# Moving the start of the output weights, the convolution's closing norm and two attention steps in a hybrid decoder trunk

## The chip, the cores and the metric

The kernel runs on one core of one Trainium2 chip. The metric is the device time of one execution in microseconds (us). Of several runs the median is taken.

## What is computed

The reference is a trunk of two layers over x of 512 positions by 1024 features. Each layer adds half a SwiGLU feed-forward part, then a mixer, then half a second feed-forward part:

```python
for l in range(DEPTH):                                   # DEPTH = 2
    x = x + 0.5 * swiglu(rms_norm(x, ffn1_norm[l]), ...)  # 1024 -> 2816 -> 1024
    h = rms_norm(x, mix_norm[l])
    a, g, q, k, v = jnp.split(h @ w_in[l], splits, axis=-1)       # 512 columns each
    conv_out = conv_module(a, g, conv_w[l], conv_b[l], conv_norm[l])
    ...
    diff_out = diff_attention(q, k, v, rel_bias, lam, lam_init, subln_norm[l])
    x = x + jnp.concatenate([conv_out, diff_out], axis=-1) @ w_out[l]
    x = x + 0.5 * swiglu(rms_norm(x, ffn2_norm[l]), ...)

def conv_module(a, g, conv_w, conv_b, conv_norm):
    u = a * jax.nn.sigmoid(g)
    y = <causal depthwise convolution of u, width 31> + conv_b
    return jax.nn.silu(rms_norm(y, conv_norm))            # norm over the 512 channels

def diff_attention(q, k, v, ...):     # 4 heads, two maps of width 64 each, values of width 128
    # per block of 128 queries: s = q k / sqrt(d) + bias, causal; p = softmax(s)
    a = p[:, :, 0] - lam * p[:, :, 1]
    o = a @ v;  o = rms_norm(o, subln_g) * (1.0 - lam_init)
```

## The kernel before

All matrix products are made in three passes of a shorter float format. A number is split into a high part (a copy in that format) and a low part (the number less its high part), and a product is high by high, low by high and high by low, added in one bank of PSUM. The helper `mm3` issues the three (L172, L175, L176). For the weights, `chunk` loads 512 KB with a DMA of SyncE's queue into a slot of the ring `wraw` (five slots), and `parts_of` has ScalarE make the high part (`whi`, L100) and VectorE, or GpSimd where the call names it, the low part (`wlo`, L101); each of these rings has four slots. x lies feature by feature in eight tiles of 128 features by 512 positions.

The eight banks of PSUM are shared out by tag: two for `mm`, two for `sc`, two for `po`, one for `tp`, one for `y`. A scheduler orders the instructions of each engine after the program is written; only instructions handed to `tc.keep_in_program_order` keep their places among each other. So the order of the calls below is a wish, and the built order can differ.

The mixer of a layer goes so:

- `conv_in` makes the four channel tiles `us[c]` of the convolution (a tile is 128 channels by 512 positions), and `project` and `to_features` make keys `kt` and queries `qz`.
- `project_values(j)` makes the values of 128 positions with 24 matmuls (L630 to L632), four such blocks; ScalarE scales them into `vv` (L633).
- `conv_taps(c, n)` does the 31 taps of channel tile c. Of these, n are made by ScalarE (products, L671) and GpSimd (sums, L672), the rest by VectorE (L686), by `POOL_TAPS = (31, 0, 0, 10)`. VectorE joins both parts (L689), and `conv_square` adds the squares into `csum` (ScalarE L658, GpSimd L659).
- `attend(n)` is a pipeline over 16 steps, four blocks of 128 queries from the last to the first, with four heads each. At call n, step n makes two score matmuls (L717, in banks `sc` and `po`; 512, 384, 256 or 128 columns wide), VectorE adds the bias and takes the minimum (L721), ScalarE the exponentials (L725), and VectorE joins both maps (L728, L730, L731). Step n - 2 is transposed (TensorE L738, ScalarE L740), step n - 3 multiplied with the values (L747). With the last head of a block come its norm (`se` L754, ScalarE L756, VectorE `so` L758, GpSimd L759 and the root L223, VectorE `ov` L762), and with step n - 5 its way out (`block_out`: transposes L774, high part L776, low part L777).
- `conv_finish` closes the convolution branch: `rows_rstd` turns the channel sums into rows (TensorE L230, VectorE L234, L235, GpSimd's root L223), `spread` copies them to all partitions (TensorE L243, ScalarE `rb` L247); then for each channel tile GpSimd multiplies (L697), ScalarE takes tanh (L699), VectorE forms the swish (L700), ScalarE the high part `acth` (L701) and VectorE the low part `actl` (L702).
- The output projection multiplies half 0 (the conv channels) for all eight output tiles of 512 columns, then half 1 (attention) in two parts of 256 columns. The results take the banks `sc` and `po` in turn, after the scores, and VectorE adds them to x (L828). The weights come by `chunk(wout[l, half, m // 2], G)`: their low parts are GpSimd's.

What decides the order around the change is written in the mixer's last part:

```python
for n in range(2):
    attend(n)
    project_values(NT - 1 - 2 * n)
    project_values(NT - 2 - 2 * n)
for c in range(CT):
    conv_taps(c, POOL_TAPS[c])
for n in range(2, len(steps) + 5):
    attend(n)
conv_finish()
```

## Time and profile before

| what | value |
|---|---|
| median of 3 runs | 1792.57 us (1792.52 to 1795.35) |
| the profiled execution's own time | 1792.75 us |
| its span | 1791.0 us |
| granted TensorE clock | 1.00 |
| TensorE busy | 1783.5 us |
| VectorE busy | 1203.1 us |
| ScalarE busy | 895.0 us |
| GpSimd busy | 643.1 us |

The span is the stretch of the profiled execution from its first to its last instruction; the time beside it also has what lies around it. A row of a timeline gives the start in us from the start of the span, the duration in us, the engine, the line and operation, the tile written and those read, the shape and the count of instructions taken together; in brackets stand the idle time before it and what ended it. PE is TensorE, DVE is VectorE, ACT is ScalarE, POOL is GpSimd. Matmuls overlap in the pipeline, so their pace is read from start to start. Instructions of the other engines overlap by some hundredths of a us too. Line numbers in the rows are those of the kernel before.

### The profile page before, as it was taken

Reading aid. Unit: us, or ns where it says so; the run is one execution under the profiler, and the core shown is the slowest. Engines: PE = TensorE matmul, PEld = TensorE weight load, DVE = VectorE, ACT = ScalarE, POOL = GpSimd, SP = SyncE. Lnnn points to the kernel's source line nnn. Section 1 sums busy time; section 2 is a strip of 40 time slices with the busy share of each in tenths; the row PEclk is TensorE's granted clock in tenths of the full one; section 3 lists DMA queues with packets and bytes.
Section 4 is the critical chain, followed back from the end, with each engine's and each line's share of the span. In section 5 each row is a group of like instructions: output and inputs, shape, how many; then the busy total and the mean of one; then the engine's idle time right before and its main releaser. Section 6 shows DMA issues by size and latency. Waiting matters only on the chain.

```text
span 1791.0 us, 28372 instructions
## 1 busy us (share of the span) xinstructions
PE 1783.5 (100%) x10861; PEld 1591.8 (89%) x10861; DVE 1203.1 (67%) x1849; ACT 895.0 (50%) x1479; POOL 643.1 (36%) x453
## 2 busy tenths in 40 slices
PE   9999999999999999999999999999999999999999
PEld 7899899888788899899888998998887888998997
DVE  7877476568867767477566665765788587674762
ACT  6455265445845455265433643654558354552651
POOL 2242232269843133133102412312798331322420
PEclk9999999999999999999999999999999999999999
DMA  7366466322212367367333654663231133664651
GB/s 247 107 174 185 112 179 175 119 93 94 71 48 84 94 165 191 104 171 193 102 95 99 169 168 121 174 182 118 71 116 50 48 107 96 169 172 112 182 150 59
DMA packets 111721, 231.24 MB, mean 129 GB/s; under 512 B 12151, under 2 KB 33414, under 8 KB 111584
## 3 DMA queue, kind: packets, MB, share of 16 engines
q1 hardware_dynamic: 91488, 191.93, 33.5%
q0 software_dynamic: 19808, 37.33, 12.5%
q8 instruction: 85, 1.39, 0.3%
q14 instruction: 52, 0.43, 0.1%
q10 hardware_dynamic: 288, 0.16, 0.0%
HBM read 227.26 MB, written 3.42 MB: 129 GB/s over the span
## 4 chain that ended last, share of the span: by engine, by line
PE 95%; DVE 4%; DMA 0%; issue 0%; ACT 0%; SPq 0%; DVEq 0%; ACTq 0%
PE ps_pair L384 38%; PE ps_d L172 9%; PE ps_d L176 9%; PE ps_d L175 9%; PE ps_pair L176 5%; PE ps_pair L175 5%; PE ps_pair L172 5%; PE ps_pair L601 2%; PE ps_pair L600 2%; PE ps_pair L602 2%; PE ps_out L175 1%; PE ps_out L176 1%; PE ps_out L172 1%; PE ps_sc L717 1%; DVE actl L261 1%; PE ps_v L632 1%
## 5 line engine op out<-in xcount | busy, mean ns | idle before, releaser
L100 ACT ACTIVATE whi<-wraw 128x512 fp32r<-128x512 f32 (+2 forms) x600 | 466.0, 801 | 611.3 <-PE ps_pair L384 226.4
L101 DVE TENSOR_TENSOR wlo<-wraw,whi 128x512 fp32r<-128x512 f32 (+2 forms) x557 | 521.6, 959 | 219.6 <-ACT whi L100 214.6
L384 PE MATMUL ps_pair<-acth,wlo 128*128 128x256 f32 x1088 | 308.3, 283 | 0.0
L384 PE MATMUL ps_pair<-actl,whi 128*128 128x256 f32 x1088 | 308.3, 283 | 0.0
L384 PE MATMUL ps_pair<-acth,whi 128*128 128x256 f32 x1088 | 308.3, 283 | 0.0
L175 PE MATMUL ps_d<-hl,whi 128*128 128x512 f32 x704 | 274.3, 390 | 0.0
L176 PE MATMUL ps_d<-hh,wlo 128*128 128x512 f32 x704 | 273.1, 389 | 0.0
L172 PE MATMUL ps_d<-hh,whi 128*128 128x512 f32 x704 | 269.3, 390 | 0.0
L384 PE MATMUL ps_pair<-th,wlo 128*128 128x256 f32 x816 | 231.2, 283 | 0.0
L384 PE MATMUL ps_pair<-tl,whi 128*128 128x256 f32 x816 | 231.1, 283 | 0.0
L384 PE MATMUL ps_pair<-th,whi 128*128 128x256 f32 x816 | 231.1, 283 | 0.0
L150 POOL DMA_DIRECT2D wraw<-in_gu x68 | 81.9, 1204 | 412.9 <-DMA wraw<-in_gu 143.2
L155 POOL TENSOR_TENSOR wraw<-wraw 128x512 f32<-128x512 f32 x68 | 104.9, 1543 | 331.0 <-DMA wraw<-in_gu 239.8
L384 PEld LDWEIGHTS ps_pair<-acth,whi 128*128 128x128 f32 x1088 | 209.1, 192 | 0.3
L384 PEld LDWEIGHTS ps_pair<-actl,whi 128*128 128x128 f32 x1088 | 209.1, 192 | 0.3
L384 PEld LDWEIGHTS ps_pair<-acth,wlo 128*128 128x128 f32 x1088 | 209.1, 192 | 0.0
L484 DVE SCALAR_TENSOR_TENSOR x<-ps_d,x 128x512 f32<-128x512 f32 x96 | 64.8, 689 | 179.0 <-PE ps_d L176 178.7
L175 PE MATMUL ps_pair<-actl,whi 128*128 128x512 f32 x448 | 175.0, 391 | 0.3 <-DVE actl L261 0.2
L176 PE MATMUL ps_pair<-acth,wlo 128*128 128x512 f32 x448 | 174.6, 391 | 0.0
L172 PE MATMUL ps_pair<-acth,whi 128*128 128x512 f32 x448 | 174.0, 393 | 0.2 <-ACT whi L100 0.2
L384 PEld LDWEIGHTS ps_pair<-th,whi 128*128 128x128 f32 x816 | 156.7, 192 | 0.6
L384 PEld LDWEIGHTS ps_pair<-tl,whi 128*128 128x128 f32 x816 | 156.7, 192 | 0.7
(169 smaller groups left out, 3247.1 us busy)
## 6 DMA issues: line engine op xcount, KB each, us to landing
wraw<-in_gu SPq DMA_DIRECT2D x208, 256.0 KB, 4.0
wraw<-in_gu SPq DMA_DIRECT2D x104, 512.0 KB, 3.7
wraw<-in_gu POOLq DMA_DIRECT2D x68, 512.0 KB, 5.7
wraw<-in_wqkv SPq DMA_DIRECT2D x24, 512.0 KB, 3.6
wraw<-in_dn SPq DMA_DIRECT2D x84, 128.0 KB, 3.0
wraw<-in_dn SPq DMA_DIRECT2D x32, 256.0 KB, 3.2
wraw<-in_wag SPq DMA_DIRECT2D x16, 512.0 KB, 3.6
wraw<-in_wout SPq DMA_DIRECT2D x16, 512.0 KB, 3.6
```

What stands on the lines that cost most here:

```text
L100: S.activation(hi, raw, AF.Copy)
L101: (eng or V).tensor_tensor(out=lo, in0=raw, in1=f32(hi), op=ALU.subtract)
L150: nc.gpsimd.dma_start(two.rearrange("p (b c) -> p b c", b=2), u[:, h[0]].unsqueeze(1).broadcast_to([P, 2, 512]), accum_op=ALU.add)
L155: G.tensor_tensor(more[:, h[0]], two[:, h[1]], whole[:, h[0]], op=ALU.add)
L172: first = T.matmul(ps, wh, xh, start=start, stop=False)
L175: T.matmul(ps, wh, xl, start=False, stop=False)
L176: T.matmul(ps, wl, xh, start=False, stop=stop)
L384: mm = T.matmul(ps, l, r, start=first and i == j == 0, stop=False, skip_group_check=True)
L484: V.scalar_tensor_tensor(x[:, m, :], ps, 0.5, x[:, m, :], op0=ALU.mult, op1=ALU.add)
L600: T.matmul(ps[n], xh[:, t], wh, start=k == 0, stop=False)
L601: T.matmul(ps[n], xh[:, t], wl, start=False, stop=False)
L602: T.matmul(ps[n], xl[:, t], wh, start=False, stop=k == KT - 1)
```

## The change

In the changed kernel:

- The calls of `attend` and `project_values` alternate otherwise: the third step (`attend(2)`) comes ahead of the last value block, the fourth (`attend(3)`) behind it and ahead of the conv taps.
- The first four chunks of the output weights (half 0) are asked for by `next_wo`, with low parts on GpSimd that are kept in program order: the first inside `conv_taps` of the last channel tile (behind its taps), the second behind `rows_rstd`, the third and fourth behind `conv_finish`.
- `rows_rstd` for the conv norm is called ahead of `attend(4)`, and `conv_finish` behind `attend(8)`, instead of both at the end.
- The tanh result goes into the PSUM bank `y` instead of an SBUF tile.
- `se` is made by ScalarE (a square with a scale) instead of VectorE.

With the added lines, the lines of the mixer move down by 2 to 19: L697 becomes L701, L699 L703, L700 L704, L702 L706, L717 L721, L828 L847.

```diff
@@ -93,17 +93,19 @@
         dt = F32 if "raw" in tag else F32R
         return wp.tile([P, n], dt, tag=tag, name=tag, bufs=RING[tag])
 
-    def parts_of(raw, hi, lo, eng=None, first=False):
+    def parts_of(raw, hi, lo, eng=None, first=False, pin=False):
         if first:
             V.tensor_scalar(hi, raw, 1.0, None, op0=ALU.mult)
         else:
             S.activation(hi, raw, AF.Copy)
-        (eng or V).tensor_tensor(out=lo, in0=raw, in1=f32(hi), op=ALU.subtract)
-
-    def chunk(src, eng=None):
+        low = (eng or V).tensor_tensor(out=lo, in0=raw, in1=f32(hi), op=ALU.subtract)
+        if pin:
+            tc.keep_in_program_order(low)
+
+    def chunk(src, eng=None, pin=False):
         raw, hi, lo = ring("wraw"), ring("whi"), ring("wlo")
         nc.sync.dma_start(raw, src)
-        parts_of(raw, hi, lo, eng)
+        parts_of(raw, hi, lo, eng, pin=pin)
         return hi, lo
 
     def by_halves(src):
@@ -658,7 +660,7 @@
                     S.activation(sq, y, AF.Square)
                     G.tensor_tensor(csum, csum, sq, op=ALU.add)
 
-            def conv_taps(c, n):
+            def conv_taps(c, n, then=None):
 
                 wc = _AT["conv_w"] + c * TAPS
                 yp = None
@@ -685,17 +687,19 @@
                 for t in range(n + 1 if n else 1, TAPS):
                     V.scalar_tensor_tensor(ys[c] if t == PAD and not n else y, us[c][:, t : t + SEQ],
                                            pars[l][:, wc + t : wc + t + 1], y, op0=ALU.mult, op1=ALU.add)
+                if then is not None:
+                    then()
                 if n:
                     V.tensor_tensor(ys[c], y, yp, op=ALU.add)
                 conv_square(c, ys[c])
 
-            def conv_finish():
-                rcv = spread(rows_rstd(csum, CC, "c")[0], "rb")
+            def conv_finish(rcv):
+                rcv = spread(rcv, "rb")
                 for c in range(CT):
                     z = ys[c]
                     hg = ghalf[l][:, c : c + 1]
                     G.tensor_tensor(z, z, rcv, op=ALU.mult)
-                    th = mt.tile([P, SEQ], F32, tag="gl", name="th", bufs=1)
+                    th = bank("y", "ps_th")
                     S.activation(th, z, AF.Tanh, scale=hg)
                     V.scalar_tensor_tensor(z, th, 1.0, z, op0=ALU.add, op1=ALU.mult)
                     S.activation(ch[:, c, :], z, AF.Copy, scale=hg)
@@ -751,7 +755,7 @@
                 po = pos[i]
 
                 se = small.tile([P, HEADS], F32, tag="se", name="se")
-                V.scalar_tensor_tensor(se, sums[i][:, 0, :], VD * EPS, sums[i][:, 0, :], op0=ALU.mult, op1=ALU.mult)
+                S.activation(se, sums[i][:, 0, :], AF.Square, scale=math.sqrt(VD * EPS))
                 sq = tmp.tile([P, SEQ], F32, tag="sq", name="sq")
                 S.activation(sq, po, AF.Square)
                 so = small.tile([P, HEADS], F32, tag="so", name="so")
@@ -803,21 +807,36 @@
             nc.sync.dma_start(bias, skew[0])
             row["bias"] = bias
 
-            for n in range(2):
+            attend(0)
+            project_values(3)
+            project_values(2)
+            attend(1)
+            project_values(1)
+            attend(2)
+            project_values(0)
+            attend(3)
+
+            wo = []
+
+            def next_wo():
+                wo.append(chunk(wout[l, 0, len(wo)], G, pin=True))
+
+            for c in range(CT):
+                conv_taps(c, POOL_TAPS[c], next_wo if c == CT - 1 else None)
+            rcv = rows_rstd(csum, CC, "c")[0]
+            next_wo()
+            for n in range(4, len(steps) + 5):
                 attend(n)
-                project_values(NT - 1 - 2 * n)
-                project_values(NT - 2 - 2 * n)
-            for c in range(CT):
-                conv_taps(c, POOL_TAPS[c])
-            for n in range(2, len(steps) + 5):
-                attend(n)
-            conv_finish()
+                if n == 8:
+                    conv_finish(rcv)
+                    next_wo()
+                    next_wo()
 
 
 
             for half, t in ((0, slice(0, SEQ)), (1, slice(SEQ // 2, SEQ)), (1, slice(0, SEQ // 2))):
                 if t.stop == SEQ:
-                    w = [None] * 4
+                    w = [None] * 4 if half else wo
                 for m in range(KT):
                     if w[m // 2] is None:
                         w[m // 2] = chunk(wout[l, half, m // 2], G)
```

## The prediction

> **What bounds the kernel now.** I read the page first, then busy time by windows, then the timelines of the engines around the one place where TensorE waits.

> ```profile
> span 1791.0 us, 28372 instructions
> PE 1783.5 (100%) x10861; PEld 1591.8 (89%) x10861; DVE 1203.1 (67%) x1849; ACT 895.0 (50%) x1479; POOL 643.1 (36%) x453
> PE 95%; DVE 4%; DMA 0%; issue 0%; ACT 0%; SPq 0%; DVEq 0%; ACTq 0%
> ```

> TensorE is busy all along and carries 95% of the chain that ended last; VectorE carries 4%. The change takes no matmul away, so it can gain only where TensorE runs below its rate. The windows show where (columns: window, us, then PE, PEld, DVE, ACT, POOL busy, clock, DMA share, GB/s):

> ```profile
> 470.00:484.00 14.00, 14.00 (x72) 9.85 (x71) 9.34 (x30) 12.72 (x29) 13.59 (x9) 1.00 0.52 150
> 484.00:511.00 27.00, 25.89 (x157) 20.55 (x156) 26.33 (x93) 22.45 (x67) 12.40 (x13) 1.00 0.01 2
> 1373.00:1400.00 27.00, 25.88 (x157) 20.51 (x156) 25.98 (x94) 22.71 (x68) 12.55 (x14) 1.00 0.02 7
> ```

> From 484 to 511 of layer 0, and at the same place of layer 1, VectorE is full (26.33 of 27.00): attention's masks and differences share it with the end of the convolution branch. Just before, it is a third idle while GpSimd is full (13.59 of 14.00). How far TensorE falls back is read from its steps, start to start:

> ```profile
> 471.45 1.88 PE L717 MATMUL ps_sc<-kt,qz 128*128 128x512 f32 x4
> 473.16 0.60 PE L738 MATMUL ps_at<-ident,e 128*128 128x128 f32 x4
> 473.60 2.53 PE L717 MATMUL ps_sc<-kt,qz 128*128 128x512 f32 x6
> 476.40 1.06 PE L747 MATMUL ps_o<-vv,at 128*128 128x128 f32 x8
> 477.29 1.46 PE L717 MATMUL ps_sc<-kt,qz 128*128 128x384 f32 x4
> 478.58 0.61 PE L747 MATMUL ps_o<-vv,at 128*128 128x128 f32 x4
> 485.48 0.60 PE L717 MATMUL ps_sc<-kt,qz 128*128 128x256 f32 x2
> 485.92 0.83 PE L747 MATMUL ps_o<-vv,at 128*128 128x128 f32 x6
> 499.61 0.50 PE L172 MATMUL ps_out<-acth,whi 128*128 128x512 f32 x1
> 509.06 0.50 PE L175 MATMUL ps_out<-actl,whi 128*128 128x512 f32 x1
> 511.59 0.39 PE L172 MATMUL ps_out<-acth,whi 128*128 128x512 f32 x1
> 511.82 0.39 PE L175 MATMUL ps_out<-actl,whi 128*128 128x512 f32 x1
> ```

> A score matmul is two records: 0.86 us at 512 columns (471.45 to 473.16 is two), 0.645 at 384, 0.44 at 256, by size 0.22 at 128. A transpose takes 0.11 (0.44 for four), a `ps_o` product 0.22 (two records; 0.89 for eight records), an output matmul 0.23. Between 471.45, where the last value block ends, and 509.06, the low part of the fourth conv channel, stand 4 + 8 + 8 + 8 scores of the four sizes (13.8), 58 transposes (6.3), 76 `ps_o` records (8.4) and 20 output matmuls (4.6): 33.1 us in 37.6. So 4.5 us per layer is lost, 9.0 in all: that bounds any gain.

> **The change, part by part.** *Attention order.* In the built order of the changed kernel the third step's two scores and the first step's transposes stand inside the last value block; the fourth step's stand behind it all the same. TensorE's work moves and does not shrink: the value block ends at 471.45 + 1.72 + 0.44 = 473.6. Up to the first output matmul follow two scores of 512 (1.72), eight of 384 (5.16), eight of 256 (3.5), five of 128 (1.1), 30 + 12 transposes (4.6) and 32 `ps_o` products (7.0): 23.1 us, so at full rate it stands at 496.7, and the low part of the fourth channel 3.6 us later, at 500.3. What VectorE delivers later than that is the new loss.

> *Conv branch earlier.* The tanh products L697 (after: L701) now follow step 8 instead of the end. VectorE's steps from the first product with tanh to the last low part come from this stretch of before, again start to start:

> ```profile
> 496.93 0.42 DVE L721 CUSTOM_DVE_ANT_0 ps_sc<-ps_sc,bias 128x256 f32<-128x256 f32 x1
> ...
> 497.26 0.68 DVE L758 TENSOR_REDUCE so<-sq 128x4 f32<-128x512 f32 x1
> 497.86 0.28 DVE L721 CUSTOM_DVE_ANT_0 e<-ps_sc,bias 128x128 f32<-128x128 f32 x1
> ...
> 498.07 0.69 DVE L700 SCALAR_TENSOR_TENSOR yp<-th,yp 128x512 f32<-128x512 f32 x1
> 498.67 0.30 DVE L721 CUSTOM_DVE_ANT_0 ps_sc<-ps_sc,bias 128x128 f32<-128x128 f32 x1
> ...
> 498.88 0.16 DVE L728 RECIPROCAL r<-sums 128x1 f32<-128x1 f32 x1
> ...
> 499.15 0.28 DVE L730 TENSOR_SCALAR c<-r,nlam,sums 128x1 f32<-128x1 f32 x1
> 499.46 0.49 DVE L731 SCALAR_TENSOR_TENSOR e<-ps_sc,c,e 128x256 f32<-128x256 f32 x1
> 499.86 0.74 DVE L702 SCALAR_TENSOR_TENSOR actl<-yp,ghalf,acth 128x512 fp32r<-128x512 f32 x1
> 500.52 0.69 DVE L700 SCALAR_TENSOR_TENSOR u<-th,u 128x512 f32<-128x512 f32 x1
> ```

> A step is the duration less some 0.08: tanh product L700 0.60, low part L702 0.66, `so` 0.60, L731 0.40, mask L721 0.34 at 256 and 0.21 at 128, reciprocal with factor 0.31. In the new order the mask that frees the bank for the first output matmul ends a list of three L700 (1.80), two L702 and an equal L777 (1.98), one `so` (0.60), two L731 (0.80), two masks of 256 (0.68), four of 128 (0.84) and three pairs (0.93): 7.6 us after the stretch starts. Another L731, two L702, L700, `ov` (as `so`) and a pair make 10.9 to its end.

> *When it starts.* GpSimd's and ScalarE's steps:

> ```profile
> 477.38 1.28 POOL L672 TENSOR_TENSOR yp<-yp,prod 128x512 f32<-128x512 f32 x1
> 478.61 2.38 POOL L101 TENSOR_TENSOR wlo<-wraw,whi 128x1024 fp32r<-128x1024 f32 x1
> 488.85 0.20 POOL L759 TENSOR_TENSOR so<-so,se 128x4 f32<-128x4 f32 x1
> 492.30 1.01 POOL L223 TENSOR_TENSOR rs_y<-rowv,mhalf 128x4 f32<-128x4 f32 x1 [2.15 <-DVE rowv L235]
> 496.04 3.67 POOL L697 TENSOR_TENSOR u<-u,rb 128x512 f32<-128x512 f32 x3
> 472.23 1.05 ACT L100 ACTIVATE whi<-wraw 128x1024 fp32r<-128x1024 f32 x1
> 473.18 0.71 ACT L671 ACTIVATE prod<-u,par 128x512 f32<-128x512 f32 x1
> 496.70 0.73 ACT L699 ACTIVATE th<-yp,ghalf 128x512 f32<-128x512 f32 x1
> ```

> In ScalarE's new order the last tap's product stands behind the last value block's scaling and one high part of the output weights: 473.6 + 0.15 + 0.6 + 1.0 + 0.6 = 476.0. GpSimd adds it by 477.3, does the first pinned low part by 479.7 (the last channel's square sum is queued behind it, and waits for ScalarE's square, behind five masked steps, until about 481 anyway), and the sum is whole at 482.1. TensorE's list has the rows of the norm 11.1 of the 23.1 us down, at 484.7, so no wait is added there. VectorE has them at 485.0, and with a sum (0.6), a mask (0.4) and two small steps is done at 486.3. GpSimd's queue then holds the root (1.0), the second pinned low part (2.4), `so` (0.2) and the root of the first attention block (1.0), to 491.05, and the first L697 (1.25), to 492.3. Tanh 0.6 later gives the start, 492.9. Queued behind that low part are the root of attention and all four L697. From the other side, the last 256 wide scores ahead of the stretch (5.6 us of TensorE's list remain after them) end at 491.1; a wake of 0.15 and two masks make 491.95 the earliest. I take 492.9, the later of the two.

> *The pinned low parts.* The first two lie in 477 to 490, where VectorE waits for scores anyway. The third and fourth run right behind the four L697, so beside L702, which has two inputs in SBUF. What this does is seen elsewhere:

> ```profile
> 542.03 0.75 DVE L261 SCALAR_TENSOR_TENSOR actl<-x,par,acth 128x512 fp32r<-128x512 f32 x1 [0.79 <-ACT acth L260]
> 545.17 1.80 DVE L261 SCALAR_TENSOR_TENSOR actl<-x,par,acth 128x512 fp32r<-128x512 f32 x1
> 544.68 1.74 POOL L273 TENSOR_TENSOR ssum<-ssum,sq 128x512 f32<-128x512 f32 x1 [13.95 <-ACT sq L269]
> ```

> Alone the low part L261 takes 0.75; started at 545.17, inside a GpSimd sum that ends at 546.42, it ends at 546.97, 0.55 behind that sum. It was held until the sum ended. [...]

> With hold: VectorE reaches the first L702 2.5 us after the start, at 495.4, inside the fourth L697 (492.3 + 3 × 1.25 = 496.05), and leaves at 496.6. The third low part begins behind it and ends at 498.9; VectorE reaches the second L702 2.06 later, at 498.66, and leaves at 499.45. L731, L700, a pair and two masks later (1.73) the bank is free, at 501.2, TensorE goes on at 501.35: 4.65 late against 496.7. The third L702 is held to 502.3 by the fourth low part (ends at 501.75); `ov` then waits for GpSimd's root until 503.0; the fourth L702 ends at 504.7, and 504.85 is 4.55 late against 500.3. TensorE is not late twice: the larger counts.

> *Tanh in a bank.* L700 with one operand in a bank should take a step of 0.66 as L702 does against 0.60 (bounds: 0 to 0.06 each); the holds hide most, I take 0.05 in all. [...] It also leaves L700 one SBUF input, so that L697 and low parts no longer hold it.

> *`se` on ScalarE.* Eight small VectorE instructions go and eight come on ScalarE, which has room in the stretch (22.45 of 27.00); VectorE waits for scores where two of them stood. I take 0, from −0.1 to +0.2 a layer. SP's load order is unchanged: 0.

> Sum per layer: 4.65 + 0.05 = 4.7 lost instead of 4.5, so +0.2, twice: +0.4. The profiled execution took 1792.75; 1793.15 there is 1793.0 against the median 1792.57, which lies 0.18 under it. Measurement of this kernel can tell about 0.2%, 3.6 us, from no change, so this is none.

> **Rivals.** *Slower: the third low part gets ahead of the first L702.* The margin is 0.65 us: if VectorE reaches it after 496.05 instead of 495.4, it finds the third low part running and is held until 498.4 + 0.55. The second follows at 501.0, held to 501.85 by the fourth; the bank is free at 503.6, 7.0 late: +2.5 a layer, 1797.6. For it: ScalarE's part between tanh and the high part is as full as VectorE's. Against: both engines start from the same first L697. A chain 0.7 later on top gives 1799.

> *Faster: half the stall goes.* GpSimd's queue loses three of four low parts ahead of the norm, and VectorE has 4.7 us idle between 470 and 484 to fill. 2.25 a layer, 1788.1. It needs the stretch to start at 490.4; the scores allow 491.95, at best 3.0 lost, 1789.6. So it needs TensorE's list to be shorter than I count.

> *The order does nothing:* the fourth step stays behind the value block, and the stall stays as it is at 1792.6. That is in the forecast's band.

> **How the numbers follow.** No change 0.48, slower by holds 0.35, faster 0.17. The range goes from the faster case (1788) to the slower one with its late chain (1799); the forecast's own is 1789.6 to 1796.

> **What would show it.** Right: first output matmul near 501.3, fourth L702 near 504.7, first L702 about 1.2 us long, TensorE's loss per layer near 4.7. L702 of over 2 us shows the slower rival; a first output matmul before 499 shows the faster one. If the tanh of the first channel comes well before or after 492.3, my GpSimd walk is wrong.

## The result: 0.5% slower, by a held VectorE and a slower TensorE clock

The changed kernel takes 1801.45 us (median of 6 runs, 1799.97 to 1804.0) against 1792.55 us: a ratio of 1.0048 (95% interval 1.0038 to 1.0059). The forecast was 1793.0, within 0.2% of before, with a range up to 1799; the measured time lies above it. The profiled execution took 1800.38 us. One execution further on, the profiled one of e3_filled_wait, ran at a clock of 0.556 from end to end and took 2955.5 us; the ratio given there leaves it out.

From its page, and its busy time by windows at the place where the prediction looked (us, then PE, PEld, DVE, ACT, POOL busy, granted clock, DMA share, GB/s):

```profile
span 1798.6 us, 28354 instructions
PE 1785.7 (99%) x10861; PEld 1595.9 (89%) x10861; DVE 1200.1 (67%) x1841; ACT 895.3 (50%) x1487; POOL 643.5 (36%) x453
PE 97%; DVE 3%; issue 0%; ACT 0%; DVEq 0%; ACTq 0%
484.00:511.00 27.00, 23.03 (x135) 19.91 (x134) 23.85 (x75) 19.83 (x60) 15.60 (x12) 0.81 0.19 59
1373.00:1400.00 27.00, 23.06 (x139) 19.35 (x138) 25.03 (x79) 22.56 (x68) 18.87 (x14) 0.87 0.27 79
```

The chain says less than one would think: VectorE's share fell from 4% to 3%, though the kernel got slower, at least in part because time at a slow clock is booked as TensorE's own. The windows tell it. TensorE is idle for 4 us of the 27 instead of 1.1, and its granted clock, 1.00 in the kernel before, is 0.81 and 0.87 here. Both losses are seen in TensorE's timeline:

```profile
496.58 0.38 PE L742 MATMUL ps_at<-ident,e 128*128 128x128 f32 x2
499.64 0.80 PE L721 MATMUL ps_sc<-kt,qz 128*128 128x128 f32 x2 [2.68 <-DVE mn L725]
...
503.20 0.79 PE L174 MATMUL ps_out<-acth,whi 128*128 128x512 f32 x1 [0.39 <-DVE mn L725]
503.80 0.63 PE L177 MATMUL ps_out<-actl,whi 128*128 128x512 f32 x1
504.22 0.63 PE L178 MATMUL ps_out<-acth,wlo 128*128 128x512 f32 x1
504.65 0.63 PE L174 MATMUL ps_out<-acth,whi 128*128 128x512 f32 x1
...
509.38 0.39 PE L177 MATMUL ps_out<-actl,whi 128*128 128x512 f32 x1
509.60 0.39 PE L178 MATMUL ps_out<-acth,wlo 128*128 128x512 f32 x1
```

TensorE waits 2.68 us for a mask of VectorE. Behind the wait an output matmul takes a step of 0.43 us (504.22 to 504.65) where it took 0.23, until 508.5: its instructions run at about half speed for 9 us. The first output matmul stands at 503.20, 6.5 late against 496.7; the low part of the fourth channel at 509.38, 9.1 late against 500.3. In the kernel before, the same matmul was 4.5 late against the place that full rate would have given it there. In layer 1 the wait is the same, the slow stretch 6 us. VectorE's and GpSimd's rows say why TensorE waited:

```profile
493.18 0.69 DVE L704 SCALAR_TENSOR_TENSOR yp<-ps_th,yp 128x512 f32<-128x512 f32 x1 [0.26 <-ACT ps_th L703]
495.79 2.58 DVE L706 SCALAR_TENSOR_TENSOR actl<-yp,ghalf,acth 128x512 fp32r<-128x512 f32 x1
498.30 0.68 DVE L704 SCALAR_TENSOR_TENSOR u<-ps_th,u 128x512 f32<-128x512 f32 x1
```

```profile
491.10 1.27 POOL L701 TENSOR_TENSOR yp<-yp,rb 128x512 f32<-128x512 f32 x1
492.34 3.18 POOL L701 TENSOR_TENSOR u<-u,rb 128x512 f32<-128x512 f32 x3
495.49 5.10 POOL L101 TENSOR_TENSOR wlo<-wraw,whi 128x1024 fp32r<-128x1024 f32 x2
```

The third low part began at 495.49, VectorE reached the first low part of the conv branch 0.3 us later and was held: 2.58 us for an instruction of 0.74. The GpSimd instruction itself, the first of the two in that row, ended at 497.83, the held one 0.54 us behind it.

### The profile page after: what moved, and what is told of

Read it like the earlier page. It is cut to its first block, busy times and chain, and to the rows that moved or that the text cites. A ratio compares the mean times of both kernels' runs of the same rounds, so it can differ in the third digit from the quotient of the medians.

```text
span 1798.6 us, 28354 instructions
## 1 busy us (share of the span) xinstructions
PE 1785.7 (99%) x10861; PEld 1595.9 (89%) x10861; DVE 1200.1 (67%) x1841; ACT 895.3 (50%) x1487; POOL 643.5 (36%) x453
## 4 chain that ended last, share of the span: by engine, by line
PE 97%; DVE 3%; issue 0%; ACT 0%; DVEq 0%; ACTq 0%
PE ps_pair L386 38%; PE ps_d L178 9%; PE ps_d L174 9%; PE ps_d L177 9%; PE ps_pair L178 5%; PE ps_pair L177 5%; PE ps_pair L174 5%; PE ps_sc L721 2%; PE ps_pair L602 2%; PE ps_pair L604 2%; PE ps_pair L603 2%; PE ps_out L174 1%; PE ps_out L177 1%; PE ps_out L178 1%; DVE actl L263 1%; PE ps_v L634 1%
## 5 line engine op out<-in xcount | busy, mean ns | idle before, releaser
L100 ACT ACTIVATE whi<-wraw 128x512 fp32r<-128x512 f32 (+2 forms) x600 | 465.5, 801 | 606.5 <-PE ps_pair L386 226.3
L101 DVE TENSOR_TENSOR wlo<-wraw,whi 128x512 fp32r<-128x512 f32 (+2 forms) x557 | 515.9, 949 | 224.6 <-ACT whi L100 219.9
```

The costliest lines, as they stand in the source:

```text
L100: S.activation(hi, raw, AF.Copy)
L101: low = (eng or V).tensor_tensor(out=lo, in0=raw, in1=f32(hi), op=ALU.subtract)
```

## Experiments

**The held instruction.** My theory was that of VectorE and GpSimd the one that begins first holds the other to its end, and that the clock falls behind the wait that follows. The first experiment takes the two low parts out of that place.

```diff
                 if n == 8:
                     conv_finish(rcv)
+                if n == 14:
                     next_wo()
                     next_wo()
```

> The changed kernel with its third and fourth pinned low parts asked for behind step 14 instead of behind the four tanh products, so that on GpSimd they stand behind the root of the third attention block. Theory (the hold, then the clock): the first L706 takes about 0.75 instead of 2.58 us, TensorE's wait of 2.68 us falls under 1 us, no stretch runs at half clock, and TensorE is 4.3 to 4.9 us late per layer: 1791.5 to 1793.5. Rival (the moved order, tanh in the bank and se are what costs): about 1800 as the changed kernel.

Measured: 1795.35 us, ratio 1.0017 (1.0008 to 1.0026): 6.1 us of the 8.9 are gone, but not all. VectorE and TensorE:

```profile
495.94 0.74 DVE L706 SCALAR_TENSOR_TENSOR actl<-yp,ghalf,acth 128x512 fp32r<-128x512 f32 x1
```

```profile
497.95 0.49 PE L721 MATMUL ps_sc<-kt,qz 128*128 128x128 f32 x2 [0.84 <-DVE mn L725]
499.88 0.49 PE L721 MATMUL ps_sc<-kt,qz 128*128 128x128 f32 x2 [0.99 <-DVE e L735]
```

```profile
484.00:511.00 27.00, 24.02 (x155) 20.60 (x154) 24.60 (x87) 21.50 (x65) 10.57 (x10) 1.00 0.07 22
1373.00:1400.00 27.00, 24.36 (x154) 21.06 (x153) 24.10 (x84) 21.08 (x64) 10.57 (x10) 0.94 0.10 34
```

The hold is gone (0.74) and the lateness in layer 0 is close to that of the forecast's likeliest case: the first output matmul stands at 501.73 and the low part of the fourth channel at 505.05, against 501.35 and 504.85. But waits of 0.84 and 0.99 us are left close together; in layer 0 the clock stayed at 1.00, in layer 1 it is 0.94. The expectation had full clock and at most 1793.5, and was wrong there.

The second cuts the third and fourth low part into two instructions of 512 columns each:

```diff
-        low = (eng or V).tensor_tensor(out=lo, in0=raw, in1=f32(hi), op=ALU.subtract)
+        cut = 512 if pin == 2 else raw.shape[-1]
+        for c0 in range(0, raw.shape[-1], cut):
+            s = slice(c0, c0 + cut)
+            low = (eng or V).tensor_tensor(out=lo[:, s], in0=raw[:, s], in1=f32(hi)[:, s], op=ALU.subtract)
...
```

> The changed kernel with its third and fourth low parts made in two instructions of 512 columns each instead of one of 1024. Theory (a GpSimd instruction that began first holds L706 to its end): the first L706 falls from 2.58 to about 1.5 us (the rest of 1.25, then 0.55), TensorE's longest wait from 2.68 to about 1.6 us; with the clock at half behind it some 1797, without it 1793 to 1795. Rival (a shared access only slows both): the first L706 stays near 2.6 us, and the time near 1800.

Measured: 1798.96 us, ratio 1.0034 (1.0021 to 1.0046). The first low part on VectorE (its line is L709 here):

```profile
495.82 1.51 DVE L709 SCALAR_TENSOR_TENSOR actl<-yp,ghalf,acth 128x512 fp32r<-128x512 f32 x1
```

```profile
498.60 0.49 PE L724 MATMUL ps_sc<-kt,qz 128*128 128x128 f32 x2 [1.61 <-DVE mn L728]
500.69 0.79 PE L724 MATMUL ps_sc<-kt,qz 128*128 128x128 f32 x2 [1.15 <-DVE e L738]
```

Same start, a GpSimd instruction half as long, 1.51 instead of 2.58: the first half ended at 496.78 and VectorE's instruction 0.55 us behind it, so the hold lasted to the end of the one GpSimd instruction that began first, as the prediction read it from L261 (0.55 behind the sum's end). The clock fell all the same, to 0.87 in both layers, behind 1.61 and 1.15 us of waiting (the record at 500.69 is already long, 0.79). The time is 2 us over what was expected with a fallen clock.

The third test turns the order of arrival around by adding work: a GpSimd product whose result is not used, ahead of the third low part (`row["rb"]` is the tile of the norm's rows, kept by one more line in `conv_finish`).

```diff
                     conv_finish(rcv)
+                    scr = mt.tile([P, SEQ], F32, tag="csq", name="scr", bufs=1)
+                    tc.keep_in_program_order(
+                        G.tensor_tensor(scr[:, :256], row["rb"][:, :256], row["rb"][:, :256], op=ALU.mult))
                     next_wo()
```

> The changed kernel with one more GpSimd instruction (a product of 128x256 into an unused tile, some 0.65 us, its result is not used) pinned between the fourth tanh product and the third low part. It only puts the low parts 0.65 us later, so that VectorE reaches the first L706 (495.8) ahead of the third low part (496.1 instead of 495.5). Theory (who begins first holds the other to its end): the first L706 falls from 2.58 to 0.8 to 1.0 us, the low part waits instead, TensorE has no wait over 1.3 us and runs at full clock for most or all of it; 1793 to 1796, although work was added. Rival (GpSimd's load beside VectorE is what costs): 1801 to 1803.

Measured: 1796.79 us, ratio 1.0024 (1.0014 to 1.0034): 4.7 us faster than the changed kernel, with more work.

```profile
495.90 0.86 DVE L707 SCALAR_TENSOR_TENSOR actl<-yp,ghalf,acth 128x512 fp32r<-128x512 f32 x1
```

```profile
495.60 0.60 POOL L835 TENSOR_TENSOR scr<-rb 128x256 f32<-128x256 f32 x1
496.17 5.58 POOL L101 TENSOR_TENSOR wlo<-wraw,whi 128x1024 fp32r<-128x1024 f32 x2
```

VectorE now waits only for the short product (it ended at 496.20, the held instruction 0.56 behind it), and the two low parts are held instead (5.58 against 5.10). The clock is 0.94 in both layers, behind waits of 0.95 and 1.02, and the time is 0.8 us over the range that was expected.

**The clock.** This test fills TensorE's wait and leaves VectorE's hold as it is.

```diff
-                for j in range(i + 1):
+                for j in [j for _ in range(13 if (i, h) == (1, 1) else 1) for j in range(i + 1)]:
                     t = slice(j * P, (j + 1) * P)
                     T.transpose(pt[:, t], maps[i, h][:, t], ident)
```

> The changed kernel with the two transposes of one 256 wide step (the tenth) repeated 12 times more, 24 extra transposes of 0.11 us that write the same data again, queued just ahead of TensorE's wait of 2.68 us in each layer. It does not take the hold away. Theory (half of the loss is the clock that falls behind the wait): the wait is filled, the steps behind it go at full rate, the granted clock is 1.00, and the loss per layer falls from 9.4 and 7.9 to about 6.5: 1795 to 1797. Rival (the slow steps come from the work behind the wait itself, or from the hold alone): steps stay doubled, time at or over 1800.

Measured: 1798.77 us, ratio 1.0035 (1.0023 to 1.0047). The trace of this run shows nothing of the wait, so the kernel ran again for another:

> The kernel of e3_filled_wait once more, for a trace at full clock. Theory: the waits of VectorE and the 2.5 us hold of the first L706 are there, no step of TensorE is doubled, and what is left of the loss (some 7.9 us per layer by the time of 1798.8) is waiting and the repeated transposes that stick out of the wait. Rival: doubled steps are there all the same.

Measured: 1798.7 us; the profiled execution took 1798.09.

```profile
496.42 3.00 PE L742 MATMUL ps_at<-ident,e 128*128 128x128 f32 x26
501.46 0.49 PE L721 MATMUL ps_sc<-kt,qz 128*128 128x128 f32 x2 [2.03 <-DVE e L735]
...
503.26 0.39 PE L177 MATMUL ps_out<-actl,whi 128*128 128x512 f32 x1
503.49 0.39 PE L178 MATMUL ps_out<-acth,wlo 128*128 128x512 f32 x1
```

```profile
495.63 2.60 DVE L706 SCALAR_TENSOR_TENSOR actl<-yp,ghalf,acth 128x512 fp32r<-128x512 f32 x1
```

```profile
484.00:511.00 27.00, 24.27 (x170) 21.70 (x169) 24.72 (x77) 19.93 (x61) 16.85 (x14) 1.00 0.20 59
1373.00:1400.00 27.00, 24.27 (x170) 21.38 (x169) 25.18 (x82) 21.76 (x65) 16.80 (x13) 1.00 0.24 80
```

The hold is there (2.60), a wait of 2.03 is left, the output matmuls step 0.23, and the clock is 1.00 in both layers. With the hold but without the slow clock the low part of the fourth channel stands at 507.03 in this trace, 2.2 us ahead of the changed kernel's 509.38 (the trace runs 0.16 earlier: its held L706 begins at 495.63 instead of 495.79). One thing besides the fill differs: behind it the built order puts the `ps_o` products that stood at 500.23 behind a transpose, at 502.00. In both kernels TensorE goes on only when VectorE's L735 is done, at about 501.4 to 501.5.

One stalled matmul at the start of the second feed-forward part of layer 1 serves as a mark, first in the kernel before, then with the filled wait:

```profile
1450.76 0.50 PE L175 MATMUL ps_pair<-actl,whi 128*128 128x512 f32 x1 [0.16 <-DVE actl L261]
```

```profile
1454.76 0.50 PE L177 MATMUL ps_pair<-actl,whi 128*128 128x512 f32 x1 [0.16 <-DVE actl L263]
```

There the hold, with whatever else the change costs at full clock, has cost 4.0 us over both layers. In the changed kernel the same matmul stands at 1458.42, 7.7 later than before, and its span grew by 7.6; that leaves 3.6 us for the clock in the profiled pair. The filled kernel's own span grew by 5.3: it loses 1.3 us behind the mark, far from the change. One wait of 0.86 us for a low part (at 1681.70) is part of that; why it came stays open. Without those 1.3 us the profiled time of 1798.09 would lie at the upper end of the range expected, 1795 to 1797. By the medians the fill saves 2.7 us.

**The other parts by themselves.** First the bank for tanh and `se` on ScalarE, in the kernel before:

```diff
-                    th = mt.tile([P, SEQ], F32, tag="gl", name="th", bufs=1)
+                    th = bank("y", "ps_th")
...
-                V.scalar_tensor_tensor(se, sums[i][:, 0, :], VD * EPS, sums[i][:, 0, :], op0=ALU.mult, op1=ALU.mult)
+                S.activation(se, sums[i][:, 0, :], AF.Square, scale=math.sqrt(VD * EPS))
```

> The kernel before with two small parts of the change alone: the tanh result in the PSUM bank and se on ScalarE. Orders of calls and low parts stay as before. Theory (these parts cost nothing by themselves): 1792.7 within 1.5 either way. Rival (they are what keeps e1_lows_late behind the kernel before): 1794 to 1796.

Measured: 1792.23 us, ratio 0.9997 (0.9988 to 1.0006). They cost nothing.

Then the order of attention steps and value blocks:

```diff
-            for n in range(2):
-                attend(n)
-                project_values(NT - 1 - 2 * n)
-                project_values(NT - 2 - 2 * n)
+            attend(0)
+            project_values(3)
+            project_values(2)
+            attend(1)
+            project_values(1)
+            attend(2)
+            project_values(0)
+            attend(3)
             for c in range(CT):
                 conv_taps(c, POOL_TAPS[c])
-            for n in range(2, len(steps) + 5):
+            for n in range(4, len(steps) + 5):
```

> The kernel before with the new order of attention steps and value blocks alone: norm and conv_finish stay behind all attention steps, low parts as before, tanh in SBUF, se on VectorE. Theory (the order moves TensorE's work and gains nothing): 1791.5 to 1794. Rival (the order is what costs): 1795 or more.

Measured: 1795.51 us, ratio 1.0016 (1.0007 to 1.0025), at a clock of 1.00 in both windows: the rival holds, the order alone, with the norm late, costs 2.8 us. In this kernel tanh lies in SBUF, and the first product with it, with two inputs there, is held by GpSimd's products (1.38 us, where the next one takes 0.69):

```profile
500.01 1.38 DVE L700 SCALAR_TENSOR_TENSOR yp<-th,yp 128x512 f32<-128x512 f32 x1
```

```profile
497.47 1.27 POOL L697 TENSOR_TENSOR yp<-yp,rb 128x512 f32<-128x512 f32 x1 [3.57 <-ACT rb L247]
```

The conv stretch also starts 1.9 us later than before (500.01 instead of 498.07), since the norm's products start at 497.47 instead of 494.81.

**A place for the low parts.** The changed kernel's GpSimd waits 3.80 us for the rows of the norm; this kernel puts the second low part there and keeps the late third and fourth:

```diff
+            next_wo()
             rcv = rows_rstd(csum, CC, "c")[0]
-            next_wo()
```

> As e1_lows_late, and the second pinned low part asked for ahead of the norm's rows instead of behind, so that GpSimd makes it while it waits for the rows (3.80 us idle there in the changed kernel). Theory: the root of the first attention block and the tanh products begin about 1 us earlier (490.1 instead of 491.1), the conv stretch on VectorE at 492.1 instead of 493.2, and TensorE is 3.2 to 3.8 us late per layer: 1789.5 to 1791.5, better than before. Rival (something else starts the stretch): the same time as e1_lows_late.

Measured: 1792.4 us, ratio 1.0002 (0.9993 to 1.001). Better than e1_lows_late by 3.0 us, and no better than before.

```profile
482.83 2.36 POOL L101 TENSOR_TENSOR wlo<-wraw,whi 128x1024 fp32r<-128x1024 f32 x1
486.65 1.02 POOL L225 TENSOR_TENSOR rs_y<-rowv,mhalf 128x4 f32<-128x4 f32 x1 [1.46 <-DVE rowv L237]
...
490.41 1.28 POOL L701 TENSOR_TENSOR yp<-yp,rb 128x512 f32<-128x512 f32 x1 [1.29 <-ACT rb L249]
```

```profile
498.39 0.89 PE L721 MATMUL ps_sc<-kt,qz 128*128 128x128 f32 x4 [1.20 <-DVE mn L725]
```

GpSimd's products began 0.7 us earlier (490.41) than in the changed kernel, but VectorE, full by then, took the first product with tanh at 493.33, not earlier than there (493.18). The theory of the expectation failed. What changed is that TensorE's longest wait is a single one of 1.20 us, and the profiled clock stays at 1.00 in both layers. Not every execution is like the profiled one: three of the eleven show a mean clock of 0.998 or 0.999 and take 1793.81 to 1794.94 us.

Three more started from it. The fourth step's softmax ahead of the last value block (`softmaxes(*steps[3])` called before `project_values(0)`):

> e4_second_low_first with the scores and softmaxes of the fourth step asked for ahead of the last value block, so that in the built order they do stand ahead of it (in the changed kernel the fourth step's scores stood behind). Theory (the scores behind the value block set the start of all that follows): VectorE gets work 2 us earlier, the conv stretch starts 0.5 to 1.5 us earlier, loss per layer 3.2 to 4.2 instead of 4.7: 1789.5 to 1791.5. Rival (ScalarE, full from 470 to 482, sets it): 1792.4 as e4_second_low_first, or later.

Measured: 1793.0 us, ratio 1.0006 (0.9997 to 1.0015): the rival. The first product with tanh starts at 493.92, later than without.

Seven instead of ten taps of the fourth channel through ScalarE and GpSimd (`POOL_TAPS = (TAPS, 0, 0, 7)`):

> e4_second_low_first with 7 instead of 10 taps of the fourth channel made by ScalarE and GpSimd, the other three by VectorE. ScalarE loses 3 products (0.6 each) of the stretch from 470 to 482 in which it is full, GpSimd 3 sums (1.25 each), VectorE gains 3 taps of 0.66 where it idles 2.1 us for ScalarE. Theory (ScalarE sets it): exponentials come 1.8 us earlier, the conv stretch starts 0.5 to 1.5 us earlier, 1789.5 to 1791.5. Rival (VectorE's load sets it): 2 us per layer more on VectorE, 1794 to 1796.5.

Measured: 1798.92 us, ratio 1.0035 (1.0023 to 1.0048), worse than its rival had it. The conv stretch does start far earlier, at 489.42, but TensorE then waits for attention, which VectorE does later:

```profile
496.18 0.70 PE L721 MATMUL ps_sc<-kt,qz 128*128 128x256 f32 x2 [1.18 <-DVE e L735]
498.22 0.71 PE L751 MATMUL ps_o<-vv,at 128*128 128x128 f32 x4 [1.12 <-ACT at L744]
```

An early start of the conv stretch was worth nothing here; since VectorE also had three more taps a layer, the run doesn't show what it would be worth by itself. TensorE is idle for 4.5 us of the 27 in layer 0 and still keeps a clock of 1.00; in layer 1 the clock is 0.94. And the old attention order with the rest of e4_second_low_first, once with the tanh products behind step 8, once behind step 10:

> e4_second_low_first with the attention order of the kernel before: low parts of the output weights pinned late, norm and tanh products behind step 8, tanh in the bank, se on ScalarE. Theory (the order costs 1.4 us a layer by itself, the early norm gives back about as much): TensorE 3.3 to 4.3 us late per layer, 1789.6 to 1791.6, better than both kernels. Rival (with the early norm the order costs nothing, since the norm is then what VectorE waits for): 1792 to 1793.

> e11_old_order_new_rest with the tanh products behind step 10 instead of 8. Theory (VectorE is full from 484 on, and its work for attention and for the conv branch only change places): within 1.5 us of e11_old_order_new_rest. Rival (an earlier conv branch lets the output projection fill TensorE's waits): 1.5 to 4 us slower than it.

Measured: 1794.01 us, ratio 1.0006 (0.9997 to 1.0014), and 1793.64 us, ratio 1.0004 (0.9995 to 1.0013). The first lies over both its theory and its rival, the second within 1.5 us of the first, as its theory had it. With the norm early the new order is not what costs: the old one in its place is no faster than e4_second_low_first. By the medians it is 1.6 us slower, but eight of its eleven executions ran at a mean clock under 1.00; the three at 1.00 took 1792.57 to 1793.08, much like e4_second_low_first. No version beat the kernel before by more than the measurement can tell. The last one shows the clock best. TensorE's two long waits are the same in both layers:

```profile
496.72 0.70 PE L721 MATMUL ps_sc<-kt,qz 128*128 128x256 f32 x2 [1.54 <-DVE e L735]
498.25 0.93 PE L721 MATMUL ps_sc<-kt,qz 128*128 128x128 f32 x4 [0.60 <-DVE mn L725]
...
1387.28 0.70 PE L721 MATMUL ps_sc<-kt,qz 128*128 128x256 f32 x2 [1.54 <-DVE e L735]
1388.80 0.89 PE L721 MATMUL ps_sc<-kt,qz 128*128 128x128 f32 x4 [0.60 <-DVE mn L725]
```

```profile
484.00:511.00 27.00, 24.41 (x147) 20.91 (x146) 24.25 (x82) 20.30 (x62) 10.85 (x12) 0.94 0.07 20
1373.00:1400.00 27.00, 24.42 (x158) 20.56 (x157) 24.44 (x84) 21.40 (x64) 11.83 (x13) 1.00 0.07 22
```

In layer 0 the clock fell behind them (0.94), in layer 1 it did not (1.00). In e11_old_order_new_rest, with the same two waits (1.54 and 0.60), it is 0.94 in both layers.

## Why the prediction was wrong

- *What bounds the kernel, and the place:* right. All the time was lost in the stretch named, per layer, by VectorE's conv branch beside attention: behind it, at the mark of the experiments, the changed kernel is already 7.7 us late, as at its end. The order costs no TensorE work, yet it is not free, as I had it: alone, with the norm late, it takes 2.8 us.
- *The walk to the start:* close. The first product with tanh stood at 493.18 (forecast 492.9), the first L706 was reached at 495.79 (495.4).
- *The hold:* right as it was read from L261. The first L706 took 0.74, 0.86, 1.51 and 2.58 us beside no GpSimd instruction and beside one of 256, 512 and 1024 columns, and the three that were held ended 0.54 to 0.56 us behind it. What failed is the margin of 0.65 us on which the likeliest case stood. I gave each L701 1.25 us, from L697's 3.67 for three. They took 3.18 for three: in before, one was held by an L700 with two SBUF inputs (1.56 us against 1.10 for the others), and with tanh in a bank that hold is gone (1.08 to 1.10 for all of them), which I wrote myself under "Tanh in a bank" and did not carry into the GpSimd walk. So the third low part began at 495.49 instead of 496.05, and VectorE came 0.4 later than walked: a margin of −0.3. Either slip alone would have left VectorE first. What came is the slower rival, with its sign (an L706 of over 2 us); its lateness at the first output matmul was forecast at 7.0 and came out at 6.5.
- *The clock:* missing in every case, and this is the step that put the time outside the range. I summed lateness, and took a microsecond of waiting as a microsecond; a slower clock was put at nothing without a reason. The slower rival's own extra came out near its forecast (2 us a layer at full clock in the trace with the wait filled, 2.5 forecast), but the waits also halved the clock behind them, 3.6 us more in the profiled pair. With the likeliest case alive (e1_lows_late) the time would have been 1795.35 and not 1793.0, in part for the same reason: its clock fell in layer 1, and in layer 0, at full clock, the first output matmul was 5.0 late where 4.65 was forecast.
- *Which part did it:* pinning the third and fourth low part behind the tanh products, 6.1 of 8.9 us. Moving the second in front of the norm's rows gives the rest back (3.0 us), not by an earlier start but with waits that left the clock up in most executions. Tanh in the bank and `se` cost nothing, as forecast; the product with tanh lasts 0.69 from the bank, as it did from SBUF, and it was held neither by an L701 (0.69 at 493.18) nor by a low part (0.68 at 498.30), so even the 0.05 was too much (L702, which I took as its model, reads no operand from a bank). The tanh itself took 0.67 to 0.70 us into the bank, against 0.71 to 0.73 into SBUF.

## What to carry to other kernels

A VectorE instruction with two SBUF inputs beside a long GpSimd instruction was here a bet on who came first, and the loser waited: VectorE 2.58 us for an instruction of 0.74, GpSimd's pair of low parts 5.58 us instead of 5.10. Before GpSimd work is moved, look at what VectorE does beside it. With the GpSimd instruction cut in half the hold fell to 1.51 us, and a VectorE instruction with one operand in a bank was not held at all (0.68 us inside a low part of the changed kernel). Where TensorE is the bound, do not only add up its waits: look at how many of them fall into the same few microseconds, and at the granted clock by windows. The 4.5 us of waits in layer 0 of e8_fewer_products, spread out, left the clock at 1.00; 1.85 us within 3.4 us in the changed kernel were followed by 10.24 us at half clock. A margin of some tenths of a us between two engines is no forecast of which comes first: a forecast margin of 0.65 came out as −0.3.

## What the runs showed of the hardware

TensorE's clock fell to half behind waits as short as 1.54 and 0.60 us (layer 0 of e12_norm_behind_ten). What follows is read from the traces of this case. Cut into windows of 0.25 us, the granted clock in the two stretches is 1.00 or 0.50, with other values only where an edge falls into a window. It fell in seven of the thirteen kernels' traces. Each stretch at 0.50 lasts 3.4 us or a whole multiple of it: three such steps in layer 0 of the changed kernel (498.21 to 508.45, 10.24 us), two in its layer 1 (6.83 us from 1392.50), two in both layers of e2_lows_in_halves, one in each of the others. The starts in the two layers lie a whole number of these steps apart: with a step of 3.413 us, a third of that 10.24, they are 262 steps apart in the changed kernel (894.29 us) and 261 in e2_lows_in_halves, e9_low_a_step_later and e11_old_order_new_rest (890.88 us). So in these four traces one row of steps fits both layers, and the cases sort by how long TensorE is idle within one step:

| trace | step (us) | TensorE idle in it | clock in the next step |
|---|---|---|---|
| e8_fewer_products | 493.18 to 496.60 | 1.41 | 1.00 |
| e12_norm_behind_ten, layer 1 | 1386.42 to 1389.83 | 1.46 | 1.00 |
| e9_low_a_step_later, layer 1 | 1386.09 to 1389.51 | 1.54 | 1.00 |
| e9_low_a_step_later, layer 0 | 498.63 to 502.04 | 1.59 | 0.50 |
| e12_norm_behind_ten, layer 0 | 495.54 to 498.95 | 1.79 | 0.50 |
| changed kernel, layer 0 | 494.80 to 498.21 | 1.85 | 0.50 |
| e2_lows_in_halves, layer 0 | 497.28 to 500.69 | 2.47 | 0.50 |

Holds between VectorE and GpSimd were seen in both directions: VectorE's low part took 2.58 us instead of 0.74 behind a GpSimd instruction that had begun first, and GpSimd's pair of low parts, 2.4 us each alone, took 5.10 us where it came first and 5.58 us where VectorE did (e9_low_a_step_later).
